# A decoder layer: half of the q latent moved into the modulation loop, late modulation sums held back by a chunk

## The chip, the core and the metric

The kernel runs on one core of a Trainium2 chip, in one launch. The metric is the time of an execution on the device in microseconds (us). Engines are named as in the profile: PE is TensorE (PEld its weight loads), DVE is VectorE, ACT is ScalarE, POOL is GpSimd, SP is SyncE, which issues all transfers here. Each engine works its instructions off in order.

## The reference

One causal decoder layer on 1024 tokens of width 1024, all in float32.

```python
mod = jax.nn.silu(c) @ w_ada[l] + b_ada[l]                    # c: (1, 1024), w_ada: (1024, 6144)
sh1, sc1, g1, sh2, sc2, g2 = jnp.split(mod, 6, axis=-1)

h = rms_norm(x, g_mix_norm[l]) * (1.0 + sc1[:, None]) + sh1[:, None]
proj = h @ w_in[l]                                            # 1024 x 2336 columns
q_lat, kv_lat, k_pe, qd, kd, vd = jnp.split(proj, SPLITS, axis=-1)   # 512, 256, 32, 512, 512, 512
...
k_pe = rope(rms_norm(k_pe, g_mla_k_pe[l])[:, :, None, :], positions)
o_mla = causal_dense_attention(q_mla, k_mla, v_mla, (MLA_NOPE + MLA_ROPE) ** -0.5)
qd = rope(rms_norm(qd.reshape(B, S, DIL_HEADS, DIL_HEAD_DIM), g_dil_q[l]), positions)
kd = rope(rms_norm(kd.reshape(B, S, DIL_HEADS, DIL_HEAD_DIM), g_dil_k[l]), positions)
o_dil = dilated_attention(qd, kd, vd)
x = x + g1[:, None] * (concat(o_mla, o_dil) @ w_o[l])
h2 = rms_norm(x, g_ffn_norm[l]) * (1.0 + sc2[:, None]) + sh2[:, None]
x = x + g2[:, None] * (conv_glu(h2 @ w_up[l]) @ w_down[l])
```

## The kernel before

The order of the instructions on each engine is made when the program is built: a planner walks the program in the order in which it is written and gives each engine the first instruction that its own model of the times has ready. The written order is thus a priority, and the order on the chip is fixed.

Every float32 product is done in three matmuls of a rounded part (`hi`) and a rest (`lo`): `mm3`, lines L102 to L104. For a chunk of weights, `split_weights` makes both parts: ACT copies `w_hi` (L91), POOL subtracts to get `w_lo` (L97, four pieces). There are two pairs of `hi` and `lo`, used in turn, and three `raw` buffers of 1 MB, which weights and late modulation chunks use in turn.

The modulation vector has 24 chunks of 256 columns of `w_ada`, 1 MB each. Eight of them (shift and scale of the first norm) are needed before any projection. The first loop, `for j in range(4)`, takes two of them per turn: a load into one of four `ada` buffers, 16 small matmuls (L213), a copy to `strip` (L215), sums over partitions by matmuls with `ones` (L223), and the result in `modc` (L224). Then `h_feats` transposes two features of the normalized `x` (L249), applies scale and shift on ACT (`hv`, L252) and makes `h_hi` and `h_lo`. `first_steps(0, w0, 0, ...)` adds these two features (k = 2j and 2j + 1) into the first 256 columns of the q latent for the first four row tiles, which are held open in four PSUM banks (`p`). After the loop come three full passes: the second 256 columns (`w1`) for the same tiles, then both halves for the last four tiles. ACT copies each result to `q_lat` (L315).

The other 16 modulation chunks are late ones. `ada_late` loads one into a `raw` buffer (L198), and DVE multiplies and adds it up in eight steps on `strip` (L205, then seven of L207); PE sums over partitions (L223, or L218 in row form for the gate) straight afterwards. They stand between the projection chunks: one before the key-value chunk, three behind it, two behind each of the other six.

The key-value chunk has 288 columns in eight tiles; ACT empties 256 of them and squares from PSUM, DVE takes the last 32 (`pe`, L449) from PSUM after the reciprocal root `r`. Then come, twice, a q chunk, a k chunk and a v chunk of 256 columns. In a q or k chunk (`rope_chunk`, below called rope chunks) each tile goes through ACT (`xn`, L357, four buffers; `sq`, L359, two buffers), DVE (`ss`, L361), POOL (`rs_r`, L119), DVE (L363), POOL (L365), DVE (L344, L345, L368) and a store. A v chunk has a copy by ACT and a store. The next stage transposes `q_lat` and `kv_lat` (L491), splits them (`ql_hi`, L492) and multiplies by `w_q_b`.

Of the kernel before, what the change touches and what calls it, by code (L numbers as in the profile page):

```python
# [8 lines left out]
F32 = mybir.dt.float32  # L9
# [3 lines left out]
AF = mybir.ActivationFunctionType  # L13
# [28 lines left out]
def hybrid_layer(ctx, tc, x, c, positions, w_ada, b_ada, g_mix_norm, w_in, g_q_lat, w_q_b, g_kv_lat, w_kv_b,  # L42
# [57 lines left out]

    def mm3(ps, a, b, first, last):
        T.matmul(ps, lhsT=a[0], rhs=b[0], start=first, stop=False)  # L102
        T.matmul(ps, lhsT=a[0], rhs=b[1], start=False, stop=False)  # L103
        T.matmul(ps, lhsT=a[1], rhs=b[0], start=False, stop=last)  # L104

# [96 lines left out]
    def ada_chunk(j, wa, row_form=False, late=False):  # L202
        st = hp.tile([P, 256], F32, tag="strip", name="strip", bufs=2)
        if late:
            V.tensor_scalar(st, wa[:, 0, :], cz[:, 0, 0:1], None, op0=ALU.mult)  # L205
            for k in range(1, KD):
                V.scalar_tensor_tensor(st, in0=wa[:, k, :], scalar=cz[:, k, 0:1], in1=st, op0=ALU.mult, op1=ALU.add)  # L207
        else:
            ps = bank("a")
            for q in range(2):  # L210
                for u in range(4):
                    k = 2 * u + q
                    T.matmul(ps[32 * u:32 * u + 32, 0:256], lhsT=cz[:, k, :], rhs=wa[:, k, :], start=(q == 0),  # L213
                             stop=(q == 1))
            V.tensor_copy(st, ps[:, 0:256])  # L215
        pm = bank("a")
        if row_form:
# [58 lines left out]
    def first_steps(u, w, hf, ks_):  # L276
        for t in range(4 * hf, 4 * hf + 4):
            if 0 in ks_:
                first[u, t] = bank("p")
        for k in ks_:  # L280
            for t in range(4 * hf, 4 * hf + 4):
                proj_step(first[u, t], w, t, 256, k)

    xs = [[], []]
    for j in range(4):
        for jj in (4 + j, j):
# [9 lines left out]
            if jj == 0:  # L296
                w0 = proj_weights(0, 256)
        if j in (1, 2):
            xr = raw_tile(2, D)
            t = 4 + 2 * (j - 1)  # L300
            nc.sync.dma_start(xr, x[t * P:(t + 2) * P, :].rearrange("(u p) d -> p u d", p=P))
            xs[1] += [x_norm(xr[:, u, :], True) for u in range(2)]
        scale_cols(gm1, j, 8, G0_MIX)
        h_feats(0, xs[0], (2 * j, 2 * j + 1))
        first_steps(0, w0, 0, (2 * j, 2 * j + 1))
        if j >= 2:
            h_feats(1, xs[1], range(4 * j - 8, 4 * j - 4))
    last_chunk = ada_last[-1]
    with tc.issue_after(last_chunk):
        w1 = proj_weights(256, 256)  # L310
    for u, w, hf in ((0, w0, 0), (1, w1, 0), (0, w0, 1), (1, w1, 1)):
        if (u, hf) != (0, 0):
            first_steps(u, w, hf, range(KD))
        for t in range(4 * hf, 4 * hf + 4):
            A.activation(q_lat[:, t, u * 256:(u + 1) * 256], first[u, t][:, 0:256], AF.Copy)  # L315

# [32 lines left out]

    def rope_chunk(c0, tabc, tabs, dst, col):  # L350
        w = proj_weights(c0, 256)
        for t in range(NT):
# [81 lines left out]
    rope_tables(ap)  # L434
    ada_late(8, True)
    w = proj_weights(C_KV, 288)
    for t in range(NT):
        junk = ap.tile([P, QL], BF16, tag="junk", name="junkl", bufs=1)
        ss = ap.tile([P, 3], F32, tag="kss", name="kss", bufs=4)
        A.activation(junk, q_lat[:, t, :], AF.Square, scale=float(QL ** -0.5), accum_out=ss[:, 2:3])  # L440
        ps = proj_mm(w, t, 288)
        A.activation(kv_lat[:, t, :], ps[:, 0:256], AF.Copy)
        A.activation(junk[:, 0:KVL], ps[:, 0:256], AF.Square, scale=float(KVL ** -0.5), accum_out=ss[:, 0:1])
        A.activation(junk[:, 0:ROPE], ps[:, 256:288], AF.Square, scale=float(ROPE ** -0.5), accum_out=ss[:, 1:2])
        r = rstd_of(ap, ss, 3, 1.0, "k2")
        V.tensor_copy(rkv_lat[:, t:t + 1], r[:, 0:1])
        V.tensor_copy(rq_lat[:, t:t + 1], r[:, 2:3])
        pe = ap.tile([P, 1, ROPE], F32, tag="pe", name="pe", bufs=2)
        V.tensor_scalar(pe[:, 0, :], ps[:, 256:288], r[:, 1:2], None, op0=ALU.mult)  # L449
        V.tensor_tensor(k_pe[:, t, :], pe[:, 0, :], mkc[:, t, :], op=ALU.mult)  # L450
# [3 lines left out]
    for t in range(NT):  # L454
        V.tensor_scalar(q_lat[:, t, :], q_lat[:, t, :], rq_lat[:, t:t + 1], None, op0=ALU.mult)
        V.tensor_scalar(kv_lat[:, t, :], kv_lat[:, t, :], rkv_lat[:, t:t + 1], None, op0=ALU.mult)
    for j in range(1, 4):
        ada_late(8 + j, True)
    for u in range(2):
        rope_chunk(C_QD + u * 256, qc, qs, qd_s, u * 256)  # L460
        ada_late(16 + 2 * u)
        ada_late(12 + 2 * u)
        rope_chunk(C_KD + u * 256, kc, ks, kd_s, u * 256)
        ada_late(17 + 2 * u)
        ada_late(13 + 2 * u)
        w = proj_weights(C_VD + u * 256, 256)
        for t in range(NT):
            ps = proj_mm(w, t, 256)
            o = ap.tile([P, 256], F32, tag="vo", name="vo", bufs=6)
            A.activation(o, ps[:, 0:256], AF.Copy)  # L470
            nc.sync.dma_start(vd_s[t, :, u * 256:(u + 1) * 256], o)
        for j in range(2):
            scale_cols(gm2, 2 * u + j, 32, G0_FFN)
            ada_late(20 + 2 * u + j)
    phA.close()
# [458 lines left out]
```

## Time and profile before

| | us |
|---|---|
| median of three runs | 1479.74 (1476.22 to 1482.23) |
| the profiled execution, its own time | 1477.43 |
| its span in the profile | 1475.6 |
| PE busy | 1419.7 (96%) |
| DVE busy | 853.7 (58%) |
| POOL busy | 652.5 (44%) |
| ACT busy | 595.9 (40%) |
| mean granted clock of PE | 0.992 |

Busy is the time in which an engine executes at least one instruction; matmuls overlap, so a busy PE says only that it did not stand still. The chunks that the change touches end at about 273 us of the span.

### The profile page before, as it was taken

The page shows a single profiled execution, that of the slowest core. Times are in us where ns is not written, and L with a number is a line of the kernel's source. Part 1 is how long each engine was busy: PE and PEld are TensorE (multiplying, and loading weights), DVE is VectorE, ACT ScalarE, POOL GpSimd, SP SyncE. Part 2 cuts the span into 40 slices and gives each one's busy share as a digit, 9 for nine tenths or more (in the row PEclk, how much of TensorE's full clock was granted, in tenths as well). Part 3 has the DMA queues.
Part 4 walks back from the last instruction along what each step waited for, and adds up shares of the span by engine and source line. Part 5 has one row for each costly group of instructions (what it writes and reads, how often), then busy time and mean ns, then how long its engine had stood idle before and what let it go on. Part 6 is the DMA issues. An engine that isn't in the chain of part 4 may idle for free.

```text
span 1475.6 us, 21548 instructions
## 1 busy us (share of the span) xinstructions
PE 1419.7 (96%) x8093; PEld 1216.4 (82%) x8093; DVE 853.7 (58%) x1785; ACT 595.9 (40%) x1118; POOL 652.5 (44%) x680
## 2 busy tenths in 40 slices
PE   6889999998999998989999999999999999999999
PEld 3789999886878786879988888888888888888887
DVE  4567888787879797973654244342434334242444
ACT  4424322477878786863434212122122222212220
POOL 3355656377756666525644233233313323232330
PEclk9999999999999999999999999999999999999999
DMA  9544364536202130014311011110111011011103
GB/s 324 184 146 126 122 208 128 166 127 197 58 21 81 30 100 29 5 48 161 125 64 57 29 57 51 36 58 29 58 58 57 29 57 57 29 58 58 57 1 114
DMA packets 118832, 125.57 MB, mean 85 GB/s; under 512 B 5186, under 2 KB 112072, under 8 KB 118600
## 3 DMA queue, kind: packets, MB, share of 16 engines
q1 hardware_dynamic: 118728, 124.20, 26.0%
q8 instruction: 64, 1.05, 0.3%
q14 instruction: 40, 0.33, 0.1%
HBM read 105.30 MB, written 18.87 MB: 84 GB/s over the span
## 4 chain that ended last, share of the span: by engine, by line
PE 67%; DVE 4%; POOL 3%; DMA 3%; issue 2%; ACT 2%; SPq 0%; DVEq 0%; POOLq 0%; ACTq 0%
PE wide L103 11%; PE wide L104 11%; PE wide L102 11%; PE d L102 5%; PE d L103 5%; PE d L104 5%; PE s L630 5%; PE o L673 4%; PE x L662 4%; DMA raw<-in_w_o_dram 2%; POOL w_lo L97 1%; PE p L102 1%; DVE pt L633 1%; PE p L103 1%; PE p L104 1%
## 5 line engine op out<-in xcount | busy, mean ns | idle before, releaser
L97 POOL TENSOR_TENSOR w_lo<-raw,w_hi 128x512 fp32r<-128x512 f32 (+2 forms) x162 | 223.5, 1410 | 315.3 <-ACT w_hi L91 315.2
L102 PE MATMUL wide<-h,w_hi 128*128 128x512 f32 x704 | 273.8, 389 | 0.7 <-ACT junkE L803 0.7
L103 PE MATMUL wide<-h,w_hi 128*128 128x512 f32 x704 | 274.0, 389 | 0.0
L104 PE MATMUL wide<-h,w_lo 128*128 128x512 f32 x704 | 273.9, 389 | 0.0
L876 DVE TENSOR_TENSOR x<-d,x 128x512 f32<-128x512 f32 x176 | 118.0, 687 | 167.5 <-PE d L104 167.4
L91 ACT ACTIVATE w_hi<-raw 128x2048 fp32r<-128x2048 f32 (+3 forms) x54 | 101.0, 1870 | 249.1 <-PE wide L103 138.8
L835 DVE SCALAR_TENSOR_TENSOR y<-wide,ccols,y 128x1023 f32<-128x1023 f32 x44 | 56.3, 1280 | 244.9 <-ACT y L834 244.9
L102 PE MATMUL p<-w_hi,h_hi 128*128 128x256 f32 (+1 forms) x576 | 165.4, 289 | 3.2 <-ACT xn L357 2.9
L103 PE MATMUL p<-w_lo,h_hi 128*128 128x256 f32 (+1 forms) x576 | 163.7, 286 | 0.0
L104 PE MATMUL p<-w_hi,h_lo 128*128 128x256 f32 (+1 forms) x576 | 161.0, 285 | 0.6 <-DVE h_lo L257 0.5
L102 PEld LDWEIGHTS wide<-h,w_hi 128*128 128x128 f32 x704 | 132.1, 188 | 28.4 <-ACT junkE L803 0.8
L104 PEld LDWEIGHTS wide<-h,w_lo 128*128 128x128 f32 x704 | 132.2, 188 | 27.4
L103 PEld LDWEIGHTS wide<-h,w_hi 128*128 128x128 f32 x704 | 132.1, 188 | 27.5 <-DVE h L761 0.2
L858 POOL TENSOR_TENSOR m_lo<-y,m_hi 128x1024 fp32r<-128x1024 f32 x22 | 52.7, 2394 | 206.1 <-ACT m_hi L857 206.1
L103 PE MATMUL d<-w_lo,m_hi 128*128 128x512 f32 x352 | 136.9, 389 | 0.0
L104 PE MATMUL d<-w_hi,m_lo 128*128 128x512 f32 x352 | 136.9, 389 | 0.0
L102 PE MATMUL d<-w_hi,m_hi 128*128 128x512 f32 x352 | 132.6, 389 | 0.0
L102 PEld LDWEIGHTS p<-w_hi,h_hi 128*128 128x128 f32 x576 | 111.0, 193 | 4.1 <-ACT xn L357 3.1
L103 PEld LDWEIGHTS p<-w_lo,h_hi 128*128 128x128 f32 x576 | 111.3, 193 | 0.1
L104 PEld LDWEIGHTS p<-w_hi,h_lo 128*128 128x128 f32 x576 | 109.2, 192 | 1.2 <-DVE h_lo L257 1.2
L669 DVE TENSOR_TENSOR pT_lo<-x,pT_hi 128x512 fp32r<-128x512 f32 (+1 forms) x160 | 98.1, 633 | 17.9 <-ACT pT_hi L668 16.9
L638 POOL TENSOR_TENSOR st<-st,negone 128x1 f32<-128x1 f32 x128 | 69.4, 548 | 84.2 <-ACT pt L637 72.9
(243 smaller groups left out, 3029.8 us busy)
## 6 DMA issues: line engine op xcount, KB each, us to landing
raw<-in_w_up_dram SPq DMA_DIRECT2D x22, 1024.0 KB, 5.2
raw<-in_w_ada_dram SPq DMA_DIRECT2D x16, 1024.0 KB, 8.2
raw<-in_w_down_dram SPq DMA_DIRECT2D x11, 1024.0 KB, 4.9
ada<-in_w_ada_dram SPq DMA_DIRECT2D x8, 1024.0 KB, 5.3
raw<-in_w_in_dram SPq DMA_DIRECT2D x8, 1024.0 KB
raw<-in_w_o_dram SPq DMA_DIRECT2D x16, 512.0 KB, 5.0
xr<-in_x_dram SPq DMA_DIRECT2D x32, 128.0 KB, 2.9
out_dram<-x SPq DMA_DIRECT2D x16, 256.0 KB, 2.5
```

Of the source, the lines that this page charges most:

```text
L91: A.activation(hi, raw, AF.Copy)
L97: G.tensor_tensor(lo[:, i:i + 2, :], raw[:, i:i + 2, :], hi[:, i:i + 2, :].bitcast(F32), op=ALU.subtract)
L102: T.matmul(ps, lhsT=a[0], rhs=b[0], start=first, stop=False)
L103: T.matmul(ps, lhsT=a[0], rhs=b[1], start=False, stop=False)
L104: T.matmul(ps, lhsT=a[1], rhs=b[0], start=False, stop=last)
L630: T.matmul(ps[:, 0:b - a], lhsT=q_[:, qs_], rhs=k_[:, a:b], start=(m == 0), stop=(m == len(terms) - 1))
L638: G.tensor_tensor(st[:, 3:4], st[:, 2:3], negone, op=ALU.pow)
L662: T.transpose(px[:, c0 + (i - i0) * P:c0 + (i - i0 + 1) * P], pr[i][:, kj * P:(kj + 1) * P], ident)
L669: V.tensor_tensor(lo[:, 0:c0], px[:, 0:c0], hi[:, 0:c0].bitcast(F32), op=ALU.subtract)
L673: T.matmul(pos[odd][:, i0 * P:], lhsT=vs[:, kj, odd, :, :], rhs=part[:, b0:b0 + n], start=(kj == 0 and part is hi), stop=(kj == last and p ...
L835: V.scalar_tensor_tensor(y[:, 1:], in0=ps[:, 0:S - 1], scalar=ccols[:, 88 + ch:89 + ch], in1=y[:, 1:], op0=ALU.mult, op1=ALU.add)
L876: V.tensor_tensor(x1s[t][:, cs], ps, x1s[t][:, cs], op=ALU.add)
```

## The change

The second 256 columns of the q latent for the first four tiles are computed inside the modulation loop, in the other half of the same four banks; its weights `w1` are loaded in the loop's second turn, behind the fourth modulation chunk. Each bank is then emptied by one copy of 512 columns. The late modulation chunks leave the key-value chunk's surroundings and are spread over the six projection chunks, three to each and one to the last, in an order written out by hand; their strips go to six buffers, and their sums are issued behind the matmuls of the next projection chunk. The weights of a projection chunk are loaded one chunk ahead. In the key-value chunk ACT copies the last 32 columns as well and squares from the copies; `kss` and `pe` get eight buffers.

```diff
+    def mm3(ps, a, b, first, last, shared=False):
+        T.matmul(ps, lhsT=a[0], rhs=b[0], start=first, stop=False, skip_group_check=shared)
...
     def ada_chunk(j, wa, row_form=False, late=False):
-        st = hp.tile([P, 256], F32, tag="strip", name="strip", bufs=2)
+        st = (ap if late else hp).tile([P, 256], F32, tag="strip", name="strip", bufs=6 if late else 2)
...
+        if late:
+            strips.append((st, j, row_form))
+        else:
+            column_sums(st, j, row_form)
+
+    strips = []
+
+    def column_sums(st, j, row_form):
         pm = bank("a")
...
     def first_steps(u, w, hf, ks_):
         for t in range(4 * hf, 4 * hf + 4):
-            if 0 in ks_:
-                first[u, t] = bank("p")
+            if u == 0 and 0 in ks_:
+                first[t] = bank("p")
         for k in ks_:
             for t in range(4 * hf, 4 * hf + 4):
-                proj_step(first[u, t], w, t, 256, k)
+                ts_ = slice(t * P, (t + 1) * P)
+                mm3(first[t][:, u * 256:(u + 1) * 256], (h_hi[k][:, ts_], h_lo[k][:, ts_]),
+                    (w[0][:, k, :], w[1][:, k, :]), u == 0 and k == 0, k == KD - 1, True)
...
                 w0 = proj_weights(0, 256)
+            if jj == 1:
+                w1 = proj_weights(256, 256)
...
         first_steps(0, w0, 0, (2 * j, 2 * j + 1))
+        if j >= 1:
+            first_steps(1, w1, 0, range(4) if j == 1 else (2 * j, 2 * j + 1))
...
-    with tc.issue_after(last_chunk):
-        w1 = proj_weights(256, 256)
-    for u, w, hf in ((0, w0, 0), (1, w1, 0), (0, w0, 1), (1, w1, 1)):
-        if (u, hf) != (0, 0):
-            first_steps(u, w, hf, range(KD))
+    for hf in range(2):
+        if hf == 1:
+            for u, w in ((0, w0), (1, w1)):
+                first_steps(u, w, 1, range(KD))
         for t in range(4 * hf, 4 * hf + 4):
-            A.activation(q_lat[:, t, u * 256:(u + 1) * 256], first[u, t][:, 0:256], AF.Copy)
+            A.activation(q_lat[:, t, :], first[t], AF.Copy)
...
-    ada_late(8, True)
     w = proj_weights(C_KV, 288)
...
+        pe = ap.tile([P, 1, ROPE], F32, tag="pe", name="pe", bufs=8)
         A.activation(kv_lat[:, t, :], ps[:, 0:256], AF.Copy)
-        A.activation(junk[:, 0:KVL], ps[:, 0:256], AF.Square, scale=float(KVL ** -0.5), accum_out=ss[:, 0:1])
-        A.activation(junk[:, 0:ROPE], ps[:, 256:288], AF.Square, scale=float(ROPE ** -0.5), accum_out=ss[:, 1:2])
+        A.activation(pe[:, 0, :], ps[:, 256:288], AF.Copy)
+        A.activation(junk[:, 0:KVL], kv_lat[:, t, :], AF.Square, scale=float(KVL ** -0.5), accum_out=ss[:, 0:1])
+        A.activation(junk[:, 0:ROPE], pe[:, 0, :], AF.Square, scale=float(ROPE ** -0.5), accum_out=ss[:, 1:2])
...
-        V.tensor_scalar(pe[:, 0, :], ps[:, 256:288], r[:, 1:2], None, op0=ALU.mult)
+        V.tensor_scalar(pe[:, 0, :], pe[:, 0, :], r[:, 1:2], None, op0=ALU.mult)
...
-    for j in range(1, 4):
-        ada_late(8 + j, True)
-    for u in range(2):
-        rope_chunk(C_QD + u * 256, qc, qs, qd_s, u * 256)
-        ada_late(16 + 2 * u)
-        ada_late(12 + 2 * u)
-        rope_chunk(C_KD + u * 256, kc, ks, kd_s, u * 256)
-        ada_late(17 + 2 * u)
-        ada_late(13 + 2 * u)
...
-            ada_late(20 + 2 * u + j)
+    late = iter((16, 12, 17, 13, 20, 8, 21, 18, 9, 14, 10, 19, 15, 11, 22, 23))
+    chunks = [(c0 + u * 256, u * 256) for u in range(2) for c0 in (C_QD, C_KD, C_VD)]
+    wn = proj_weights(chunks[0][0], 256)
+    for i, (c0, col) in enumerate(chunks):
+        w = wn
+        if i + 1 < len(chunks):
+            wn = proj_weights(chunks[i + 1][0], 256)
+        ready = list(strips)
+        strips.clear()
+        for _ in range((3, 3, 3, 3, 3, 1)[i]):
+            j = next(late)
+            ada_late(j, 8 <= j < 12)
+        if i % 3 == 2:
+            value_chunk(w, col)
+        else:
+            rope_chunk(w, *((qc, qs, qd_s), (kc, ks, kd_s))[i % 3], col)
+        for args in ready:
+            column_sums(*args)
+    for args in strips:
+        column_sums(*args)
```

## Rows read from the trace of the kernel before

**Rows 1.** The page, first part: busy us (share of the span) xinstructions.

```profile
PE 1419.7 (96%) x8093; PEld 1216.4 (82%) x8093; DVE 853.7 (58%) x1785; ACT 595.9 (40%) x1118; POOL 652.5 (44%) x680
```

**Rows 2.** Timeline of PE, 24 to 280 us: start, us, what, [idle before <-releaser].

```profile
32.13 0.61 PE L223 MATMUL a<-ones,strip 128*128 128x1 f32 x4 [0.56 <-DVE strip L215]
...
47.88 1.07 PE L213 MATMUL a<-ada,cz 128*32 128x256 f32 x16
49.40 1.32 PE L249 MATMUL x<-ident,xt 128*128 128x128 f32 x8 [0.45 <-ACT hv L252]
54.20 0.66 PE L249 MATMUL x<-ident,raw 128*128 128x128 f32 x4 [3.14 <-ACT hv L252]
...
73.43 0.70 PE L218 MATMUL a<-strip,ones 128*128 128x256 f32 x2 [1.14 <-DVE strip L207]
...
101.48 0.70 PE L218 MATMUL a<-strip,ones 128*128 128x256 f32 x2 [3.87 <-DVE strip L207]
...
116.73 0.37 PE L102 MATMUL p<-w_hi,h_hi 128*128 128x288 f32 x1 [0.33 <-DVE pe L449]
...
245.52 0.39 PE L102 MATMUL p<-w_hi,h_hi 128*128 128x256 f32 x1 [2.89 <-ACT xn L357]
...
277.91 0.44 PE L102 MATMUL p<-w_hi,ql_hi 128*128 128x384 f32 x1 [2.93 <-ACT ql_hi L492]
```

**Rows 3.** Busy time by stretches of 4 us; last three: granted clock, DMA share, GB/s.

```profile
28.00:32.00 4.00, 3.56 (x37) 2.82 (x36) 1.87 (x7) 2.30 (x4) 1.84 (x3) 1.00 1.09 378
...
52.00:56.00 4.00, 1.79 (x10) 1.56 (x11) 2.43 (x3) 1.41 (x2) 3.56 (x3) 0.88 0.12 28
56.00:60.00 4.00, 4.00 (x27) 4.00 (x27) 1.89 (x4) 2.86 (x4) 1.28 (x1) 0.70 0.70 234
...
100.00:104.00 4.00, 2.52 (x13) 2.47 (x14) 1.85 (x4) 1.59 (x1) 4.00 (x7) 0.85 0.30 89
104.00:108.00 4.00, 4.00 (x24) 4.00 (x24) 0.72 (x2) 1.03 (x5) 4.00 (x5) 0.72 1.09 361
```

**Rows 4.** Timeline of PE: first and last row of the pass's 96 matmuls.

```profile
60.58 0.36 PE L102 MATMUL p<-w_hi,h_hi 128*128 128x256 f32 x1
...
71.86 0.28 PE L104 MATMUL p<-w_hi,h_lo 128*128 128x256 f32 x1
```

**Rows 5.** Timeline of SP's queue: start, us, line, what it issues.

```profile
24.67 10.22 SPq L198 DMA_DIRECT2D ada<-in_w_ada_dram  x3
34.98 2.87 SPq L261 DMA_DIRECT2D raw<-in_w_in_dram  x1
```

**Rows 6.** Timeline of ACT, where the weights `w1` land.

```profile
46.76 1.91 ACT L91 ACTIVATE w_hi<-raw 128x2048 fp32r<-128x2048 f32 x1 [0.56 <-DMA raw<-in_w_in_dram]
```

**Rows 7.** Groups of ACT, 0 to 275 us: shapes, count, busy us, mean ns, idle before.

```profile
L440 ACT ACTIVATE junkl<-q_lat 128x512 bf16<-128x512 f32 x8 | 5.0, 631 | 0.2
```

**Rows 8.** Busy time in the first rope chunk: all of it (DVE third), then L207 alone.

```profile
129.00:152.00 23.00, 23.00 (x197) 23.00 (x197) 16.38 (x52) 8.34 (x20) 17.17 (x17) 1.00 0.25 76
...
129.00:152.00 23.00, 0.00 (x0) 1.00 0.25 76
```

**Rows 9.** Groups of DVE, 102 to 275 us: the twelve late strips of that stretch.

```profile
L207 DVE SCALAR_TENSOR_TENSOR strip<-raw,cz,strip 128x256 f32<-128x256 f32 x84 | 45.1, 575 | 0.3
...
L205 DVE TENSOR_SCALAR strip<-raw,cz 128x256 f32<-128x256 f32 x12 | 9.4, 788 | 8.5 <-DMA raw<-in_w_ada_dram 8.5
```

**Rows 10.** Timeline of ACT in the second key chunk.

```profile
245.09 0.38 ACT L357 ACTIVATE xn<-p 128x256 f32<-128x256 f32 x1 [4.80 <-POOL ro L365]
```

**Rows 11.** Timelines of DVE and POOL: a product without and beside POOL's split.

```profile
140.59 0.28 DVE L344 TENSOR_TENSOR rb<-xn,qs 128x128 f32<-128x128 f32 x1
...
156.01 5.19 POOL L97 TENSOR_TENSOR w_lo<-raw,w_hi 128x512 fp32r<-128x512 f32 x4
...
157.37 1.38 DVE L344 TENSOR_TENSOR rb<-xn,qs 128x128 f32<-128x128 f32 x1
```

**Rows 12.** Timeline of ACT at the end of the stage.

```profile
275.80 1.48 ACT L91 ACTIVATE w_hi<-raw 128x1536 fp32r<-128x1536 f32 x1 [2.51 <-DMA raw<-in_w_q_b_dram]
```

More of the change, by code (lines that the diff above doesn't have):

```diff
@@ L99, in split_weights @@
         return hi, lo
[L101 to L104, printed above, removed]
+    def mm3(ps, a, b, first, last, shared=False):
+        T.matmul(ps, lhsT=a[0], rhs=b[0], start=first, stop=False, skip_group_check=shared)
+        T.matmul(ps, lhsT=a[0], rhs=b[1], start=False, stop=False, skip_group_check=shared)
+        T.matmul(ps, lhsT=a[1], rhs=b[0], start=False, stop=last, skip_group_check=shared)
     ident = cp.tile([P, P], F32, name="ident")
@@ L348, in ada_late, with rope_chunk @@
         ada_chunk(j, ada_load(j, raw_tile(KD, 256)), row_form, True)
-    def rope_chunk(c0, tabc, tabs, dst, col):
-        w = proj_weights(c0, 256)
+    def rope_chunk(w, tabc, tabs, dst, col):
         for t in range(NT):
@@ L438, in hybrid_layer @@
         junk = ap.tile([P, QL], BF16, tag="junk", name="junkl", bufs=1)
-        ss = ap.tile([P, 3], F32, tag="kss", name="kss", bufs=4)
+        ss = ap.tile([P, 3], F32, tag="kss", name="kss", bufs=8)
         A.activation(junk, q_lat[:, t, :], AF.Square, scale=float(QL ** -0.5), accum_out=ss[:, 2:3])
         ps = proj_mm(w, t, 288)
+        pe = ap.tile([P, 1, ROPE], F32, tag="pe", name="pe", bufs=8)
         A.activation(kv_lat[:, t, :], ps[:, 0:256], AF.Copy)
-        A.activation(junk[:, 0:KVL], ps[:, 0:256], AF.Square, scale=float(KVL ** -0.5), accum_out=ss[:, 0:1])
-        A.activation(junk[:, 0:ROPE], ps[:, 256:288], AF.Square, scale=float(ROPE ** -0.5), accum_out=ss[:, 1:2])
+        A.activation(pe[:, 0, :], ps[:, 256:288], AF.Copy)
+        A.activation(junk[:, 0:KVL], kv_lat[:, t, :], AF.Square, scale=float(KVL ** -0.5), accum_out=ss[:, 0:1])
+        A.activation(junk[:, 0:ROPE], pe[:, 0, :], AF.Square, scale=float(ROPE ** -0.5), accum_out=ss[:, 1:2])
         r = rstd_of(ap, ss, 3, 1.0, "k2")
@@ L447, in hybrid_layer @@
         V.tensor_copy(rq_lat[:, t:t + 1], r[:, 2:3])
-        pe = ap.tile([P, 1, ROPE], F32, tag="pe", name="pe", bufs=2)
-        V.tensor_scalar(pe[:, 0, :], ps[:, 256:288], r[:, 1:2], None, op0=ALU.mult)
+        V.tensor_scalar(pe[:, 0, :], pe[:, 0, :], r[:, 1:2], None, op0=ALU.mult)
         V.tensor_tensor(k_pe[:, t, :], pe[:, 0, :], mkc[:, t, :], op=ALU.mult)
@@ L456, in hybrid_layer, with value_chunk @@
         V.tensor_scalar(kv_lat[:, t, :], kv_lat[:, t, :], rkv_lat[:, t:t + 1], None, op0=ALU.mult)
-    for j in range(1, 4):
-        ada_late(8 + j, True)
-    for u in range(2):
-        rope_chunk(C_QD + u * 256, qc, qs, qd_s, u * 256)
-        ada_late(16 + 2 * u)
-        ada_late(12 + 2 * u)
-        rope_chunk(C_KD + u * 256, kc, ks, kd_s, u * 256)
-        ada_late(17 + 2 * u)
-        ada_late(13 + 2 * u)
-        w = proj_weights(C_VD + u * 256, 256)
+    def value_chunk(w, col):
         for t in range(NT):
@@ L470, in hybrid_layer @@
             A.activation(o, ps[:, 0:256], AF.Copy)
-            nc.sync.dma_start(vd_s[t, :, u * 256:(u + 1) * 256], o)
-        for j in range(2):
-            scale_cols(gm2, 2 * u + j, 32, G0_FFN)
-            ada_late(20 + 2 * u + j)
+            nc.sync.dma_start(vd_s[t, :, col:col + 256], o)
+    late = iter((16, 12, 17, 13, 20, 8, 21, 18, 9, 14, 10, 19, 15, 11, 22, 23))
[18 more added lines that the diff above has]
+        column_sums(*args)
+    for j in range(4):
+        scale_cols(gm2, j, 32, G0_FFN)
     phA.close()
```

## The prediction

> **What bounds the kernel now.** I read the page first: TensorE is busy 96% of the span [rows 1], so a microsecond is won where TensorE stands still or runs slowly, and hardly anywhere else. The change touches only the first fifth of the span. So the next view is TensorE's order of time there, where each bracket gives the idle time before an instruction and what ended it [rows 2]. Between 24 and 280 us there are ten such waits of 0.3 us or more: four of 0.45 to 0.56 us in the modulation loop, 2.1 in all (the first and the last stand in the rows), 3.14 at the loop's end (behind the last modulation chunk's `hv`), 1.14 and 3.87 for a `strip` that VectorE has not finished, 0.33 for `pe`, 2.89 for `xn` in the second key chunk and 2.93 for `ql_hi` where the next stage begins. The third view is the stretches of 4 us with the granted clock [rows 3]: it is 0.88 and 0.70 behind the 3.14 wait, 0.85 and 0.72 behind the 3.87 wait, and 1.00 in the other stretches that I read up to 120 us. Between the two levels, 1.2 and 2.4 GHz, the work lost is (1 - share) x 4 us: 1.68 behind the first, 1.72 behind the second. I price the 2.89 wait alike, 4.6 us with its clock. What follows in the kernel is bound by TensorE too, so I let a microsecond won here reach the end.
>
> **The change part by part.** The number of matmuls stays the same; they move.
>
> *Sums of late strips.* Now a late chunk's two sum matmuls stand right behind its nine VectorE operations, and TensorE, in order, waits for them: 1.14 before the third projection pass, 3.87 before the key-value chunk, and the 1.72 of clock behind that [rows 2, 3]. Queued behind the waiting sums is the whole projection chunk. With six strip buffers and the sums held back until the next chunk's matmuls are out, the strip has had a chunk's time (some 22 us), and no late chunk stands before the key-value chunk any more. Minus 6.73 us. The sums themselves are paid as before.
>
> *Key-value chunk.* `pe` is copied by ACT, so a bank no longer waits for `rstd`, VectorE and the rotary tables. Gone is the 0.33 wait. Added are eight copies of 32 columns on ACT, which is far from full there; nothing for TensorE. Together with the sums: minus 7.06.
>
> *Second half of the q latent in the loop.* One pass (four tiles, eight k, three matmuls) takes from 60.58 to 71.98, 11.4 us [rows 4]. It moves to where TensorE has idle time: 2.1 + 3.14 + 1.68 of clock = 6.9 us from 24 to 60.58. Were all of it filled, the loop would end 11.4 - 6.9 = 4.5 us later and a pass of 11.4 be gone behind it: 6.9 gained. If nothing is filled, 0. Moved with it is a load of 1 MB: SyncE now issues `w1` behind the last three modulation chunks [rows 5], and it lands last, at 46.7 [rows 6]; it will go ahead of four chunks and of two loads of `x`, and these come later by 1 MB at 378 GB/s [rows 3], 2.8 us. The last chunk then lands where `w1` does now; TensorE took that chunk up at 47.88 [rows 2], so it need not start later, but earlier ones do, and TensorE then has u = 1 matmuls to do in place. Behind the last chunk only k = 6 and 7 of u = 1 remain as filler, 24 matmuls or 2.9 us, for the 5.3 us of wait and clock there: I leave 2 us unfilled, 4.9 gained. The four banks of the first half must now all be emptied before the second half starts, each 512 columns wide: a 512-wide ACT copy takes 0.63 [rows 7] while TensorE spends 0.35 on each tile of a round, three waits of 0.28, 0.8 us. Result: minus 4.1, bounds minus 6.9 and plus 2.8 (the delay paid, nothing filled).
>
> *Late chunks inside the projection loop.* Before, four run ahead of the key-value chunk and twelve from there on [rows 9]; in the change all 16 belong to the six chunks, three to each but the last. The cover for them is VectorE's free time, and that is thin. The first rope chunk had no strips and kept VectorE busy 16.4 of 23 us [rows 8]; a late chunk costs (45.1 + 9.4) / 12 = 4.5 us [rows 9]; TensorE needs 8 x 24 x 0.118 = 22.6 us for the chunk. So one strip fits, two do not quite. In the old order each key chunk had two: the first took it without a wait, the second ended in ACT waiting 4.80 for `xn` [rows 10], all four banks full, and the 2.89 [rows 2].
>
> Part of that 4.5 is a collision: beside POOL's split of the next weights, 5.19 us for four, a rotary product on VectorE takes 1.38 where it otherwise takes 0.28 [rows 11]. The Trainium skill's SBUF — State Buffer (section "SBUF: two separate sides") says that VectorE and GpSimd lock one shared pair of ports for a whole instruction and that the other blocks. The row agrees. By that rule every strip operation that meets a split waits for one POOL instruction, and more strips per chunk would speak against this change.
>
> Bounds of this term: minus 4.6, if the strips fall into the key-value and value chunks (VectorE is nearly free in a value chunk) and the old wait goes; plus 25, worked out as a rival below. Loads can start early, since the next weights are fetched a chunk ahead and three raw buffers turn over; that lets one or two strips run during the key-value chunk. I take zero: one wait such as the present one remains. Queued behind a strip on VectorE are the next tile's `ss`, then POOL's `rstd`, `xn`, and ACT's emptying of a bank.
>
> *End of the stage.* ACT stood 2.51 us in front of a weight copy whose load came late [rows 12]; it needs one of the three raw buffers that the last late chunks hold, and `ql_hi` stood behind the copy in ACT's queue. The last chunk now has one strip instead of two and the buffer comes free earlier. Of the 2.93 [rows 2] I take 1.5, since `ql_hi` must still follow the transposes; bounds 0 and 2.9.
>
> *Sum.* 7.06 + 4.1 + 0 + 1.5 = 12.66. The profiled execution took 1477.43, so 1464.8 on its own account. The median of the runs shown, 1479.74, lies 2.3 above it; I carry that over: **1467**.
>
> **The rivals.**
>
> *VectorE becomes the bound in the second pair of rope chunks.* Strip buffers allow six sums to be open, so strips of the fourth and fifth iterations can hardly start before their own chunks: six strips in q and k of the second pair, where there were four. That is two more at 4.5, plus 9.1; the first pair, with four where it had two, waits as the second pair does now, plus 4.6. Together plus 13.7: 1478.5, with 2.3 1481. For it: [rows 8, 9, 10]. Against: the value chunks can take a backlog.
>
> *The loop gains nothing.* The weights for u = 1 push the modulation chunks back and the loop is paced by them: plus 2.8 instead of minus 4.1, 1471.7, with 2.3 1474. For it: transfers run at 350 GB/s and more throughout that stretch [rows 3, 5]. Against: the last chunk waited for TensorE, not for its landing.
>
> *The held-back sums are waited for all the same,* because strips lag by more than a chunk: the 6.73 stays, 1471.5, with 2.3 1474. Against: six buffers, and the longest lag in the rows is 3.87.
>
> *Slower: three strips in every rope chunk, and VectorE sets the pace.* It needs 16.4 + 3 x 4.5 = 30.0 us where TensorE needs 22.6, 7.4 over in each of four, 29.6 less the 4.6 of today: plus 25, 1489.8, with 2.3 1492. It decides from (22.6 - 16.4) / 4.5 = 1.4 strips per rope chunk on, if value chunks take up no backlog. The port rule in SBUF — State Buffer of the Trainium skill points the same way.
>
> **How the numbers follow.** Forecast 0.50; second pair 0.22; loop gains nothing 0.13; sums still waited for 0.04; VectorE everywhere 0.11. The forecast's own range is 1459 (loop 6.9, stage end 2.9, the rope wait gone, each pushing down by 2.8, 1.4 and 4.6 from 1467, rounded up) to 1473 (neither the loop nor the stage's end gains, 5.6 up). About 0.5%, 7.4 us, is what a measurement can tell from no change: faster means below 1472.3. That takes nine tenths of the forecast and a third of the two cases at 1474, 0.51. Slower, above 1487.1, takes most of the last case and a little of the second pair, 0.12. The rest, 0.37, is within. The range 1460 to 1485 takes in all cases but the last and the outer edges.
>
> **What would show it.** Right: no TensorE wait for `strip` before the key-value chunk and a clock of 1.00 through it; that chunk starting near 91, where it now starts behind 101.48 [rows 2]; u = 1 matmuls between those of u = 0 from about 36 us on; the end of the last value chunk some 11 us earlier; at most one wait for `xn` in the rope chunks. Wrong: several waits of `xn` or `sq` for VectorE or POOL in q and k chunks, each with a clock below 1.00 behind it; modulation chunks that TensorE waits for; weights of the next chunk landing late because a strip held a raw buffer.

## The result and the profile after

The changed kernel takes 1490.33 us (median of six, 1486.54 to 1493.01) where the kernel before takes 1480.11 (median of six): ratio 1.0070, 95% interval 1.0048 to 1.0092. It is slower by some 10 us; the forecast was 1467. The profiled execution took 1487.8, its span is 1485.7. Line numbers of the changed kernel are 8 to 23 higher here: `hv` is L260, the sums L226 and L231, `modc` L232, `xn` L369.

The page's first line, beside [rows 1]: TensorE's busy share did not move.

```profile
PE 1423.3 (96%) x8093; PEld 1221.7 (82%) x8093; DVE 847.7 (57%) x1785; ACT 595.4 (40%) x1118; POOL 657.6 (44%) x680
```

TensorE in order of time, beside [rows 2]:

```profile
33.55 1.32 PE L257 MATMUL x<-ident,xt 128*128 128x128 f32 x8 [1.13 <-ACT hv L260]
...
47.09 0.61 PE L231 MATMUL a<-ones,strip 128*128 128x1 f32 x4 [1.30 <-DVE strip L215]
...
62.15 1.11 PE L257 MATMUL x<-ident,raw 128*128 128x128 f32 x6 [2.57 <-ACT hv L260]
...
93.34 0.32 PE L337 MATMUL x<-ident,cr 88*128 88x88 f32 x2
93.44 0.38 PE L102 MATMUL p<-w_hi,h_hi 128*128 128x288 f32 x1
...
159.99 0.39 PE L102 MATMUL p<-w_hi,h_hi 128*128 128x256 f32 x1 [1.33 <-ACT xn L369]
165.45 0.38 PE L102 MATMUL p<-w_hi,h_hi 128*128 128x256 f32 x1 [2.46 <-ACT xn L369]
177.82 1.01 PE L231 MATMUL a<-ones,strip 128*128 128x1 f32 x4 [4.17 <-DVE modc L232]
...
223.80 0.95 PE L231 MATMUL a<-ones,strip 128*128 128x1 f32 x8
231.40 1.22 PE L226 MATMUL a<-strip,ones 128*128 128x256 f32 x2 [4.55 <-DVE modc L232]
262.50 0.80 PE L231 MATMUL a<-ones,strip 128*128 128x1 f32 x3 [4.68 <-DVE modc L232]
```

The stretches of 4 us, beside [rows 3] (the column behind POOL is the granted clock):

```profile
60.00:64.00 4.00, 1.83 (x11) 1.50 (x12) 2.33 (x3) 1.97 (x3) 1.37 (x2) 0.94 0.00 0
64.00:68.00 4.00, 4.00 (x23) 3.79 (x23) 2.39 (x4) 1.96 (x3) 0.59 (x1) 0.63 0.01 2
...
100.00:104.00 4.00, 4.00 (x33) 4.00 (x32) 4.00 (x10) 2.72 (x12) 2.28 (x3) 1.00 0.00 0
...
176.00:180.00 4.00, 2.18 (x10) 2.18 (x11) 4.00 (x12) 2.25 (x3) 4.00 (x5) 0.52 0.68 202
180.00:184.00 4.00, 4.00 (x24) 4.00 (x24) 4.00 (x4) 0.15 (x1) 4.00 (x4) 0.62 0.40 130
```

What the reader is to see: the key-value chunk now starts at 93.44, 8.4 us earlier than before, with no wait for a strip in front of it and the clock at 1.00. Then, in the six projection chunks, TensorE waits 1.33 + 2.46 + 4.17 + 4.55 + 4.68 = 17.2 us where it waited 2.89. With each of the last three the clock falls: 0.52 and 0.62 from 176 on, that is (0.48 + 0.38) x 4 = 3.4 us, and as much with each of the other two; with 1.7 behind the `xn` waits 12.0 in all, against 1.7. These 12.0 may not simply be added to the waits. In shorter stretches the clock is down before the wait ends, from 176.2, 230.8 and 261.5 on, so some 1.6 us of it lie inside the waits and only 10.4 are lost work. Waits and clock are then 27.6 us where they were 4.6, 23.0 more. ACT's first copy in the key-value chunk and its last in the value chunks, first before, then after, say the same: 166.0 us lie between them before and 188.9 after, so the change loses 22.9 there.

```profile
106.92 0.38 ACT L442 ACTIVATE kv_lat<-p 128x256 f32<-128x256 f32 x1 [5.34 <-PE p L104]
...
272.90 0.38 ACT L470 ACTIVATE vo<-p 128x256 f32<-128x256 f32 x1 [2.33 <-PE p L104]
```
```profile
96.90 0.38 ACT L454 ACTIVATE kv_lat<-p 128x256 f32<-128x256 f32 x1
...
285.78 0.38 ACT L473 ACTIVATE vo<-p 128x256 f32<-128x256 f32 x1 [2.34 <-PE p L104]
```

The waits name `modc`, the addition that VectorE does behind a sum. The name is a bank's, not a number's: up to three held-back sums stand in a row, `bank("a")` has two buffers, and the third sum needs the bank of the first (223.80 is two sums in eight matmuls, 231.40 the third). VectorE comes to the `modc` that frees it only behind rope work and strips of its own queue, in the second case here:

```profile
231.19 0.15 DVE L232 TENSOR_TENSOR modc<-a,cols 128x2 f32<-128x2 f32 x1
```

Why it is so late is seen at the start of the stage, in VectorE's order of time:

```profile
73.79 1.82 DVE L265 TENSOR_TENSOR h_lo<-hv,h_hi 128x512 fp32r<-128x512 f32 x1
93.69 0.34 DVE L338 COPY ccols<-x 128x176 f32<-128x176 f32 x1 [18.08 <-PE x L337]
...
95.93 0.42 DVE L408 TENSOR_TENSOR ang<-posc,invf 128x256 f32<-128x256 f32 x1
```

VectorE stands still for 18.08 us. It has reached the copy of the convolution vectors (`ccols`), which waits for two transposes (L337) that TensorE does at 93.34, behind the second half of the q latent, now one block of 22 us. The rope tables (from `ang` on) start at 95.93; in the kernel before the copy was made at 73.69 and `ang` at 83.08. The busy time of the engines from 76 to 94 us, third number VectorE's, first before, then after:

```profile
76.00:94.00 18.00, 18.00 (x152) 17.89 (x151) 13.19 (x28) 3.46 (x5) 6.01 (x4) 1.00 0.52 163
```
```profile
76.00:94.00 18.00, 18.00 (x161) 18.00 (x160) 0.31 (x2) 3.63 (x5) 5.58 (x4) 1.00 0.35 109
```

And the strips' steps from 120 to 275 us, the groups of VectorE, first before, then after: 70 become 100, 16.3 us more. One step takes no longer than before (550 ns on average, 567 before); there are more of them.

```profile
L207 DVE SCALAR_TENSOR_TENSOR strip<-raw,cz,strip 128x256 f32<-128x256 f32 x70 | 36.8, 567 | 0.1
```
```profile
L207 DVE SCALAR_TENSOR_TENSOR strip<-raw,cz,strip 128x256 f32<-128x256 f32 x100 | 53.1, 550 | 0.5
```

### The profile page after: what moved, and what is told of

It reads as the page before. It is cut to its first block, busy times and chain, and to the rows that moved or that the text cites. A ratio compares the mean times of both kernels' runs of the same rounds, so it can differ in the third digit from the quotient of the medians.

```text
span 1485.7 us, 21548 instructions
## 1 busy us (share of the span) xinstructions
PE 1423.3 (96%) x8093; PEld 1221.7 (82%) x8093; DVE 847.7 (57%) x1785; ACT 595.4 (40%) x1118; POOL 657.6 (44%) x680
## 4 chain that ended last, share of the span: by engine, by line
PE 67%; DVE 6%; POOL 3%; issue 3%; ACT 2%; DMA 2%; SPq 0%; DVEq 0%; POOLq 0%; ACTq 0%
PE wide L103 11%; PE wide L104 11%; PE wide L102 11%; PE d L104 5%; PE d L103 5%; PE d L102 5%; PE o L696 4%; PE s L653 3%; PE x L685 3%; PE p L102 1%; DVE pt L656 1%; DMA raw<-in_w_o_dram 1%; POOL w_lo L97 1%; PE p L103 1%; PE p L104 1%
## 5 line engine op out<-in xcount | busy, mean ns | idle before, releaser
L103 PE MATMUL wide<-h,w_hi 128*128 128x512 f32 x704 | 274.0, 389 | 0.0
```

The lines of the kernel that those rows point to most:

```text
L103: T.matmul(ps, lhsT=a[0], rhs=b[1], start=False, stop=False, skip_group_check=shared)
```

## The experiments

Three theories stood against each other: the two banks make the waits; three strips in a chunk make VectorE late whatever the banks do; VectorE is late because of the 18 us at `ccols`. All runs together, each against runs of the kernel before on the same chip; e10 has six executions, the others twelve. The ratio with its interval is not the quotient of the two medians and differs from it by up to 0.0018 (e8), so differences of 2 or 3 us between runs are weak unless both agree. "Waits" are TensorE's of over 0.5 us from 120 to 270 us, "v ends" is the end of the last value copy; both come from a single profiled execution of each run. Waits ahead of 120 us are not in the column: behind 76 us, the kernel before has 3.87, e3 2.21, e5 0.80, e6 4.12, e7 0.54, e9 1.22 and e13 3.26.

| run | median, before | ratio (95%) | waits | v ends |
|---|---|---|---|---|
| before | | | 2.9 | 273.3 |
| changed kernel | 1490.33, 1480.11 | 1.0070 (1.0048 to 1.0092) | 17.2 | 286.2 |
| e1 x banks | 1484.75, 1480.23 | 1.0026 (1.0000 to 1.0053) | 8.7 | 273.6 |
| e2 strips moved | 1483.43, 1480.23 | 1.0025 (1.0010 to 1.0039) | 12.9 | 277.6 |
| e3 loop alone | 1480.84, 1480.23 | 1.0011 (0.9995 to 1.0026) | 10.8 | 278.3 |
| e4 loop, key-value | 1482.57, 1480.23 | 1.0016 (0.9996 to 1.0036) | 10.4 | 274.0 |
| e5 early copy | 1482.31, 1479.37 | 1.0006 (0.9983 to 1.0029) | 13.9 | 281.8 |
| e6 e4 + early copy | 1482.05, 1479.37 | 1.0006 (0.9983 to 1.0029) | 5.1 | 272.9 |
| e7 e5 + x banks | 1480.18, 1479.37 | 1.0006 (0.9972 to 1.0040) | 3.5 | 271.6 |
| e8 e5 + strips moved | 1479.30, 1479.37 | 0.9982 (0.9958 to 1.0006) | 8.6 | 275.3 |
| e9 all three | 1477.90, 1478.55 | 0.9994 (0.9976 to 1.0012) | 8.2 | 275.2 |
| e10 no loop part | 1486.87, 1478.55 | 1.0053 (1.0036 to 1.0070) | 13.1 | 281.4 |
| e11 no loop, banks, moved | 1475.28, 1478.55 | 0.9977 (0.9967 to 0.9986) | 8.2 | 270.3 |
| e12 e11, early strips | 1480.13, 1479.03 | 1.0006 (0.9990 to 1.0022) | 11.7 | 275.2 |
| e13 e12 + loop part | 1481.23, 1479.03 | 1.0013 (0.9998 to 1.0027) | 9.1 | 279.1 |

**e1: two more banks for the sums.**

```diff
-    def column_sums(st, j, row_form):
-        pm = bank("a")
+    def column_sums(st, j, row_form, tag="a"):
+        pm = bank(tag)
...
-        for args in ready:
-            column_sums(*args)
+        for n, args in enumerate(ready):
+            column_sums(*args, "ax"[n % 2])
```

> The changed kernel, but every second held-back sum goes to one of the two PSUM banks of the transposes (x), which nothing uses in the six projection chunks; the strips and their places stay. Bank theory: the waits of 4.17, 4.55 and 4.68 us come from three sums in a row on two banks, and with four banks they go, with the clock that falls behind them (3.44, 3.4 and 3.4): about 23 us faster than the changed kernel, 13 us faster than the kernel before. VectorE theory: three strips with a rope chunk ask for 30 us of VectorE in 22.6 us of TensorE, the lag stays, and the wait only moves to the xn and sq buffers: within 8 us of the changed kernel, not faster than the kernel before.

TensorE's waits in the six chunks of this run, and the next one:

```profile
161.01 0.38 PE L102 MATMUL p<-w_hi,h_hi 128*128 128x256 f32 x1 [1.46 <-ACT xn L369]
166.63 0.39 PE L102 MATMUL p<-w_hi,h_hi 128*128 128x256 f32 x1 [2.61 <-ACT xn L369]
237.44 0.58 PE L102 MATMUL p<-w_hi,h_hi 128*128 128x256 f32 x1 [3.06 <-ACT xn L369]
243.64 0.39 PE L102 MATMUL p<-w_hi,h_hi 128*128 128x256 f32 x1 [1.59 <-ACT xn L369]
275.62 0.69 PE L102 MATMUL p<-w_hi,ql_hi 128*128 128x384 f32 x1 [2.82 <-ACT ql_hi L515]
```

Each theory is half right. All three waits for `modc` are gone, 13.4 us, so they were the banks'; 4.65 us come back as `xn` in the second half, so VectorE is late as well. The last value copy ends 12.6 us earlier than in the changed kernel, but the span of the execution is only 4.0 shorter. Of the 8.6 between, 2.82 went to a wait for `ql_hi` that the changed kernel does not have and 3.4 to the clock with it; the rest I did not settle. That wait comes from VectorE as well: ACT stands 2.61 and 5.49 us in front of its last `vo` copies for stores of earlier ones, and in SyncE's queue these stores stand among those of `kd_s`, which wait for VectorE.

**e2: strips 2, 2, 4, 2, 2, 4.**

```diff
-        for _ in range((3, 3, 3, 3, 3, 1)[i]):
+        for _ in range((2, 2, 4, 2, 2, 4)[i]):
```

> The changed kernel with the strips of the six projection chunks counted 2, 2, 4, 2, 2, 4 instead of 3, 3, 3, 3, 3, 1; sums still held back one chunk, on two banks. VectorE theory: a rope chunk asks for 25.4 us instead of 30 against TensorE's 22.6, the four xn buffers cover what is left, and nearly all of the 17 us of waits and 12 us of clock in the six chunks go: 18 to 25 us faster than the changed kernel, 8 to 15 us faster than the kernel before. Bank theory: behind a chunk with two strips two banks do, and where four sums stand in a row the third waits for a modc add once: 12 to 18 us faster than the changed kernel, with one wait of 3 to 5 us at the end of the first chunk of the second half.

The ratio fell by 0.0045, 7 us, less than either theory gave. The bank wait came where the bank theory put it, behind the first chunk of the second half, with 6.76 us; but 4.16 and 1.95 us for `xn` stayed in the first half, which fewer strips should have taken away. VectorE must be late before its first rope chunk; here that is only inferred, e5 tests it.

**e3 and e4: the parts of the change without its late part.** e3 is the kernel before with the hunks of `mm3`, `first_steps` and the loop; e4 has those of the key-value chunk as well. The late chunks are as in the kernel before (cut, against the changed kernel):

```diff
-        if late:
-            strips.append((st, j, row_form))
-        else:
-            column_sums(st, j, row_form)
...
+    ada_late(8, True)
     w = proj_weights(C_KV, 288)
```

> The kernel before with only the second half of the q latent in the modulation loop (shared banks, one 512-wide copy); late chunks and key-value chunk as before. As forecast: 4.1 us faster than before. By the trace of the changed kernel, where the first half of q_lat ended 1.3 us earlier and the loop kept its waits: 0 to 2 us faster.

> The changed kernel without its late part: second half of the q latent in the loop and key-value chunk by ACT alone, but late modulation chunks in the places and with the immediate sums of the kernel before. If the late part costs what the trace shows (29 us lost in the six chunks against 4.6 before, less 8 won ahead of the key-value chunk), this kernel is 1 to 3 us faster than before. As forecast for these two parts alone it would be 4.4 us faster.

Both missed: neither is faster than before, and in both TensorE waits for VectorE in new places. The longest wait of e3 is in the key-value chunk, where the kernel before waits 0.33 [rows 2]:

```profile
125.83 0.58 PE L102 MATMUL p<-w_hi,h_hi 128*128 128x288 f32 x1 [8.05 <-DVE pe L454]
```

In e4, where ACT empties these banks alone, the lag appears later, as waits for `xn` of 3.40 and 3.50 us in the first key chunk (163.62, 170.13); a third, of 3.50, is where the kernel before has its 2.89. So the loop part makes VectorE late by itself, without a single strip moved. In e3 `ccols` is copied at 93.12 and `ang` starts at 99.98: this sent me to VectorE's rows above.

**e5: the convolution vectors early.** The block of four loads, two transposes and the copy is moved ahead of the second half of the q latent; its tile takes the place of `junk`.

```diff
-    last_chunk = ada_last[-1]
-    for hf in range(2):
-        if hf == 1:
-            for u, w in ((0, w0), (1, w1)):
-                first_steps(u, w, 1, range(KD))
...
-    cr = xp.tile([P, 4, P], F32, tag="hv", name="cr", bufs=2)
+    cr = xp.tile([P, 4, P], F32, tag="junk", name="cr", bufs=1)
...
     V.tensor_copy(ccols, pb[:, 0:176])
+    last_chunk = ada_last[-1]
+    for hf in range(2):
+        if hf == 1:
+            for u, w in ((0, w0), (1, w1)):
+                first_steps(u, w, 1, range(KD))
...
```

> The changed kernel, but the block of the convolution vectors (four loads, two transposes, the copy ccols) stands ahead of the second half of the q latent, with its tile in a place that is free by then; nothing else moves. Queue theory: the cause is VectorE's 18.08 us of idle time at 75.6 to 93.7, where the copy of L338 waits for the transposes of L337 that stand on TensorE behind 22 us of matmuls, and everything of VectorE behind it (rope tables, strips, key-value chunk) is late from there on; with the copy early, all waits of the six chunks and the clock behind them go: 20 to 25 us faster than the changed kernel, 10 to 14 us faster than the kernel before. VectorE theory: the lag comes from three strips in a chunk, so only the waits of the first half (1.33, 2.46, 4.17 and 5.2 of clock) go and those of 4.55 and 4.68 us with their 6.8 of clock stay: about 13 us faster than the changed kernel, 3 us faster than the kernel before. Bank theory: the waits for modc stay as they are: within 5 us of the changed kernel.

VectorE's order of time and then TensorE's waits in this run:

```profile
75.89 1.82 DVE L265 TENSOR_TENSOR h_lo<-hv,h_hi 128x512 fp32r<-128x512 f32 x1
77.63 0.33 DVE L330 COPY ccols<-x 128x176 f32<-128x176 f32 x1
...
83.72 0.42 DVE L408 TENSOR_TENSOR ang<-posc,invf 128x256 f32<-128x256 f32 x1 [5.75 <-DMA invf<-in_invf_dram]
```
```profile
174.69 0.61 PE L231 MATMUL a<-ones,strip 128*128 128x1 f32 x4 [2.90 <-DVE modc L232]
227.02 1.22 PE L226 MATMUL a<-strip,ones 128*128 128x256 f32 x2 [4.76 <-DVE modc L232]
258.14 1.01 PE L231 MATMUL a<-ones,strip 128*128 128x1 f32 x4 [6.25 <-DVE modc L232]
```

The 18 us are gone (5.75 us of idle time for a load remain) and with them both `xn` waits of the first half; the `modc` waits stay, 13.9 us in all. The value chunks end 4.4 us earlier. Against the changed kernel that is some 9 us by the two ratios, 7 by the medians, which none of the three theories gave: the late copy was a part of the cause, not the whole of it.

**e6 to e9: the edits together.** e6 is e4 with the early copy; e7 is e5 with the edit of e1, e8 is e5 with that of e2, e9 has all three (cut):

```diff
+    cr = xp.tile([P, 4, P], F32, tag="junk", name="cr", bufs=1)
...
+        for _ in range((2, 2, 4, 2, 2, 4)[i]):
...
+            column_sums(*args, "ax"[n % 2])
```

> The same early convolution block with the loop and the key-value chunk of the change, but late modulation chunks as in the kernel before. Queue theory: the 10.4 us of xn waits of the run without the late part and the clock behind them come from the late copy and go; the immediate sums ahead of the key-value chunk wait for their strips as before: 4 to 8 us faster than the kernel before. If the waits for xn come from the work of the chunks themselves, the time stays that of the run without the late part, 2 us slower than before.

> The early convolution block and every second held-back sum on an x bank, else the changed kernel. Queue theory: nothing is left to wait for a bank, so within 2 us of the run with the early block alone. Bank theory: 8 to 16 us faster than that run. VectorE theory: between, with the rest of the wait as xn waits in the second half.

> The early convolution block and strips counted 2, 2, 4, 2, 2, 4, else the changed kernel. Queue theory: within 2 us of the run with the early block alone. VectorE theory: the lag of the second half (14.6 us with three strips, 5.6 with two) goes too: 8 to 14 us faster than the run with the early block alone, about 12 us faster than the kernel before.

> The changed kernel with all three edits: the early convolution block, strips counted 2, 2, 4, 2, 2, 4, every second held-back sum on an x bank. The runs so far say that three causes add up: the late copy (VectorE late from the key-value chunk on), three strips per rope chunk, and two banks for more than two sums in a row. With the first two edits one wait of 8.62 us for a bank was left, with the clock behind it (about 5 us). If the causes add, it goes and the kernel is 10 to 14 us faster than the one before. Rival: the wait moves to xn once more, by 3 to 5 us with its clock, and the time stays within 3 us of the kernel before.

In e7 3.5 us of waits are left and the value chunks end at 271.6, 14.6 earlier than in the changed kernel: banks and late copy account for nearly all of the 17.2 us. The time of the whole kernel does not show which theory was right there, since four of the twelve executions of e7 took 1492 us (last section). e8 keeps a single wait of over 0.5 us, again a bank's; by the medians it is 3.0 us faster than e5, between what the two theories gave:

```profile
227.62 1.02 PE L231 MATMUL a<-ones,strip 128*128 128x1 f32 x4 [8.62 <-DVE modc L232]
```

e9 takes that one away and has 8.2 us of waits for `xn` and `vo` in its place: its rival came, the causes do not add. For `vo` a reason lies in the edit itself. TensorE's wait, then SyncE's and ACT's rows:

```profile
267.58 0.58 PE L102 MATMUL p<-w_hi,h_hi 128*128 128x256 f32 x1 [2.64 <-ACT vo L473]
```
```profile
260.85 0.38 SPq L572 DMA_DIRECT2D raw<-in_w_q_b_dram  x1
```
```profile
254.42 0.64 ACT L473 ACTIVATE vo<-p 128x256 f32<-128x256 f32 x2
265.77 1.48 ACT L91 ACTIVATE w_hi<-raw 128x1536 fp32r<-128x1536 f32 x1 [10.71 <-DMA raw<-in_w_q_b_dram]
267.16 1.19 ACT L473 ACTIVATE vo<-p 128x256 f32<-128x256 f32 x4
```

In ACT's queue the copy of the next stage's weights stands between the `vo` copies, and it waits 10.71 us for a load that SyncE issues at 260.85, at 247.30 in the changed kernel. With four strips instead of one in the last chunk the raw buffer comes free later: SyncE waits 4.5 to 6.1 us for strip steps ahead of the two loads of `w_q_b` in e2, e8, e9 and e11. ACT stands 8.9 to 10.9 us for this load in every run with strips moved (e12 and e13 too), at most 3.4 us in one piece in the others. No run moves the strips without this, so what it costs is not measured.

e6 lost e4's two `xn` waits of the first half, as the queue theory said, but is not faster: it waits 4.12 us for `q_lat` ahead of the key-value chunk, where ACT's sine for the rope tables, itself waiting 12.74 us for VectorE, stands ahead of the `q_lat` copies. All four runs, e6 to e9, lie within 0.2% of the kernel before.

**e10 and e11: no loop part.** `first_steps`, the passes and the load of `w1` as in the kernel before; e11 has the edits of e1 and e2 on top.

```diff
-        if j >= 1:
-            first_steps(1, w1, 0, range(4) if j == 1 else (2 * j, 2 * j + 1))
...
+    with tc.issue_after(last_chunk):
+        w1 = proj_weights(256, 256)
```

> The changed kernel without its loop part: the q latent as in the kernel before, key-value chunk by ACT alone and late chunks of the change. VectorE's copy of the convolution vectors then stands where it stood before (73.7 us) and its 18 us of idle time are gone. If the late copy is the main cause: 5 us or more faster than the kernel before. If three strips and two banks are enough by themselves (the run with the early block alone kept waits of 2.90, 4.76 and 6.25 us for modc): within 3 us of the kernel before.

> The run without the loop part, with strips counted 2, 2, 4, 2, 2, 4 and every second sum on an x bank. If the causes add and the loop itself is worth the 1.3 us by which the first half of q_lat ended earlier: 9 to 13 us faster than the kernel before, within 3 us of the run with the loop and all three edits. If the loop is worth its forecast 4.1 us, it is that much slower than that run.

e10 is 0.53% slower than the kernel before, more than either forecast allowed, though VectorE is not late (`ccols` at 72.56, `ang` at 72.83): the late part's waits for `modc` (2.69, 4.35, 6.03) are those of e5 over again. Three strips and two banks are enough by themselves. (That e5, with the same waits, has a ratio 0.5% lower was not settled; their value chunks end within 0.4 us of each other.) e11 is the only run whose whole interval lies below the kernel before, by 0.23%; the expectation was 9 to 13 us, it is 3.4. It waits 1.11 and 4.31 us for `xn` and 2.82 for `vo`. From e9 it differs in the loop part and in the place of the convolution block, which without the loop part needs no move (`ccols` at 71.92, 77.48 in e9). It is faster than e9 by 0.17%, 2.5 us, with its value chunks ending 4.9 us earlier. The intervals of the two ratios overlap, but on the same chip eight of e9's twelve executions are slower than the slowest of e11 (1476.61): the loop part costs time even with the copy early. VectorE's last `h_lo` in e9 and in e11:

```profile
75.74 1.82 DVE L265 TENSOR_TENSOR h_lo<-hv,h_hi 128x512 fp32r<-128x512 f32 x1
```
```profile
63.15 1.82 DVE L265 TENSOR_TENSOR h_lo<-hv,h_hi 128x512 fp32r<-128x512 f32 x1
```

The matmuls of the second 256 columns stand in front of the transposes of the second half's features, so VectorE ends the loop 12.6 us later, and the rope tables start at 83.44 in e9 and at 72.19 in e11.

**e12 and e13: two strips in VectorE's gap.** In e11 VectorE stood idle for 15.64 us up to 98.32, waiting for a late chunk's load, with the rope tables done. e12 puts two strips ahead of the key-value chunk (cut, against e11), e13 is the same with the loop part and the early copy.

```diff
     rope_tables(ap)
+    for _ in range(2):
+        ada_late(next(late))
     w = proj_weights(C_KV, 288)
...
-        for _ in range((2, 2, 4, 2, 2, 4)[i]):
+        for _ in range((2, 2, 3, 2, 2, 3)[i]):
...
-            column_sums(*args, "ax"[n % 2])
+            column_sums(*args, "p" if i == 0 else "ax"[n % 2])
```

> The run without the loop part, with strips 2, 2, 4, 2, 2, 4 and x banks, and now two of the strips ahead of the key-value chunk, where VectorE stood idle for 15.64 us waiting for a late chunk's load; six chunks with 2, 2, 3, 2, 2, 3, the sums of the two early strips behind the first rope chunk. VectorE theory (its total work up to the end of the last chunk sets the pace): 9 us of VectorE work less in the six chunks, so the waits that were left there (1.11, 4.31, 2.82 us, clock 3.4) shrink by half or more: 4 to 10 us faster than that run, 8 to 13 us faster than the kernel before. Rival: the strips push the rope tables back, ACT's sine stands ahead of the q_lat copies, and the key-value chunk starts later by what is won: within 2 us of that run.

> The same with the loop part (and the early convolution block). In the loop the last h_lo of VectorE ended at 75.6 us in the changed kernel against 65.0 in the kernel before, since the second half's features wait on TensorE and ACT behind the added matmuls; so rope tables and strips start 10 us later. If that is why the loop does not pay, this run is 2 to 6 us slower than the one without the loop part. If the loop failed only because of the late convolution copy, now early, this run is 1 to 4 us faster than the one without it.

e12 missed: the key-value chunk starts 2.1 us earlier than in e11 (first copy at 96.2 against 98.3), yet the run is 0.29% slower. Its waits, its VectorE and its POOL around the longest:

```profile
236.62 0.58 PE L102 MATMUL p<-w_hi,h_hi 128*128 128x256 f32 x1 [5.88 <-ACT xn L364]
264.25 0.58 PE L102 MATMUL p<-w_hi,h_hi 128*128 128x256 f32 x1 [4.66 <-ACT vo L471]
```
```profile
230.07 1.36 DVE L353 TENSOR_TENSOR rb<-xn,qs 128x128 f32<-128x128 f32 x1
...
232.49 1.56 DVE L207 SCALAR_TENSOR_TENSOR strip<-raw,cz,strip 128x256 f32<-128x256 f32 x1
```
```profile
229.96 5.21 POOL L97 TENSOR_TENSOR w_lo<-raw,w_hi 128x512 fp32r<-128x512 f32 x4
```

So VectorE's total up to the end of the stage is not all that is left. The longer wait falls where VectorE works beside POOL's split of the next weights: a product takes 1.36 us and a strip step 1.56, elsewhere 0.28 and 0.47, with the next tile's `ss` behind them. But e11 has the same meeting (two strip steps of 1.44 us at 226.52 and 227.95) ahead of a shorter wait, 4.31, so it does not tell the two runs apart. The wait for `vo` stands where it stood in e9, behind 8.94 us of ACT for the load of `w_q_b`. And the strips of e12 waited 12.2 us for their loads between 120 and 275 (eleven chunks), those of e11 9.8 (thirteen): taking the work out of one chunk did not bring the later loads forward. Why e12 is slower stays open. e13 against e12 points as e9 against e11 did (1.0013 and 1.0006, v ends at 279.1 and 275.2, the key-value chunk's first copy at 103.5 and 96.2), but their intervals overlap and the medians are 1.1 us apart.

## Why the prediction was wrong

The forecast was 1467; what came was the slower rival, 1492 with a chance of 0.11: measured 1490.3.

*Sums of late strips and key-value chunk*, minus 7.06: right. The three waits and the clock behind them are gone.

*End of the stage*, minus 1.5: right in size. The last value copy is 12.9 us later than before, the first matmul with `w_q_b` 11.1 (277.91, 288.97), so 1.8 came back; ACT's weight copy no longer waits for its load.

*Second half of the q latent in the loop*, minus 4.1: mis-sized. The first half of the q latent ends at 70.7 instead of 71.98, 1.3 us earlier; the loop's waits stayed (1.13, 1.30, 2.57 and 1.7 of clock), because the matmuls of k = 0 to 3 ran as one block from 38.85 to 44.2 and not between the waits. And the term left out what the moved work was put in front of. I followed the load of `w1` through SyncE's queue, but not the second half's block through TensorE's: the convolution transposes stand behind it, `ccols` behind them on VectorE, and all of VectorE's work of the next chunk behind that. With its late part undone (e3, e4) the change was no faster than the kernel before and showed this cost alone; with the copy early (e9 against e11) 2.5 us of it stayed, since the second half's features come later too.

*Late chunks inside the projection loop*, zero: this is the step that failed; it measured plus 22.9. I had the threshold (1.4 strips in a rope chunk) and the sum of 30.0 against 22.6 us, and still put the strips into the key-value and value chunks, where they would be free. The key-value chunk had little of VectorE left: it was busy 18.12 of 20 us from 100 to 120 (14.29 before), with rope tables that used to run earlier. And in the first value chunk VectorE, behind by then, still came to strips whose loads were late (3.07 us of idle time before 205.22). I also counted six strip buffers as the room for held-back sums and overlooked the two PSUM banks that the sums need: with two more banks waits of 13.4 us went and only 4.65 came back (e1). The term's own size is smaller than 22.9: without the loop part (e10) the stretch from ACT's first to its last copy takes 182.1 us, 16.1 more than before, so the other 6.8 are what the loop part adds to it. The collision of strips with POOL's split, which I counted against the change, did not grow by the step (550 ns, 567 before).

That the slower rival came out within 2 us is partly luck. VectorE did set the pace, but the rival's 25 us for three strips a chunk are 16.1 by themselves (e10), banks included; the waits showed mostly at `modc`, not at `xn`, and the rest came from the loop.

## What to carry to other kernels

A block that is moved or made longer has to be followed through every in-order queue that it enters: look for the small instruction behind it (here two transposes) for which another engine waits with all its work. When results are held back, count every resource that each of them holds until the slowest reader comes: PSUM banks, and the load buffers that the next stage's weights need (e9). And filling TensorE's gaps pays only if the filler does not stand in front of what feeds the engine that will set the pace next.

## What was not expected of the hardware

In the profiled execution of e7 TensorE ran at half its clock (1.2 instead of 2.4 GHz) from 344 to 400 us, from 364 on without a pause; the columns are those of [rows 3]:

```profile
344.00:364.00 20.00, 17.61 (x64) 12.12 (x65) 13.40 (x43) 14.60 (x35) 15.56 (x25) 0.54 0.45 141
364.00:384.00 20.00, 20.00 (x59) 12.93 (x57) 8.22 (x22) 7.78 (x16) 7.19 (x11) 0.50 0.07 20
384.00:400.00 16.00, 16.00 (x57) 13.61 (x57) 8.43 (x27) 8.73 (x24) 9.54 (x16) 0.50 0.00 1
```

It began behind a wait of 3.7 us, and 0.46 x 20 + 0.5 x 36 = 27 us of TensorE's work are missing in it. That execution took 1492.9 us, 12.8 above the median of its kernel, though its value chunks ended earlier than those of the kernel before. Three more of the twelve executions of e7 took as long, with a mean granted clock of 0.969 to 0.973, and so did five of the 35 of the kernel before on that chip (1490.3 to 1493.9, clock 0.976 to 0.978); no trace shows whether for the same reason. So the stretch behind 300 us is compared here by medians, not by single profiles.
